# A hybrid pooling and retention block on one core: order of the wide and narrow products in the up projection, and place of the gating multiplies

## The chip, the cores and the metric

One Trainium2 chip, one of its cores. The metric is the device time of one execution, in microseconds (us). Engines: PE is TensorE's matmuls, PEld its weight loads, DVE VectorE, ACT ScalarE, SP the engine that issues the transfers.

## What is computed

One layer of a streaming encoder on 256 tokens of width 2048, float32 throughout:

```
u = RMSNorm(h)
z = u @ W_in   -> pool | q | k | v | ret_gate | gate_pool | gate_ret
yA = PoolBranch(pool) @ P_pool
yB = (swish(ret_gate) * GroupNorm(Retention(q, k, v))) @ P_ret
h = h + (sigmoid(gate_pool) * yA + sigmoid(gate_ret) * yB) @ W_out
h = h + ConvGLU(RMSNorm(h))     up: 2048 -> 2 x 5632, causal conv of 3 and SiLU on
                                the gate half, times the other half, down: 5632 -> 2048
out = RMSNorm_final(h)
```

The change touches two places: the line of `h` that gates and adds `yA` and `yB`, and the up projection in ConvGLU.

## The kernel before, in words

Every float32 operand of a large product is split in two: `hi`, rounded to the matmul's format, and `lo`, the rest. ScalarE writes `hi` (line 82), VectorE subtracts to get `lo` (line 83). A product is then three matmuls: hi·hi, hi·lo, lo·hi.

Weights come in transfers of 1 MB (`load_split`, line 94: a raw tile of 128 x 2048, buffers: 3) and are split in two halves of 128 x 1024 each (`hi` and `lo`, 3 buffers each). `product` (line 213) makes a 256 x 512 block of a result: for each group of four 128-row steps it loads one raw tile, and per step and token block `tb` (two of 128 tokens) does the three matmuls of 512 columns (lines 90 to 92) into `ps[tb]`. The two `ps` are halves of one tile of the pool `acc`, which has two buffers.

The code is written in program order; a scheduling layer then sets the order of each engine's instructions and the semaphores, and every engine runs its own list in order. Work that TensorE should meet in between (transposes, score products) stands in the queue `side`, from which `tick()` takes one piece at set places.

*Gating (lines 459 to 486).* For each of four column blocks `nb`: the pool projection's product into `psp` (48 matmuls), then the retention projection's into `psr` (96 matmuls), then per token block three operations on VectorE: `psp` times gate (line 471), `psr` times gate (472), their sum (473). The sum is transposed later, on a tick of the next product. `psp` and `psr` take the two buffers of `acc` in turns, so the next block's `psp` needs the buffer of this block's `psp`.

*Up projection (lines 544 to 580).* 44 blocks `j`, each with two halves (gate and up, 128 columns of the result each). The weights are the stationary operand here, and the normed hidden state moves: `hview(kt)` holds 256 columns of its hi part and, beside them, 256 of its lo part. So one wide matmul of 512 columns (weight hi against both parts) and one narrow one of 256 (weight lo against the hi part) make up a step:

```python
pe.matmul(o[half], wh[:, s], both, start=kt == 0, stop=False)
pe.matmul(o[half][:, :T], wl[:, s], both[:, :T], start=False, stop=False)
```

A half-block is 16 such steps into one bank `o[half]`: 16 wide (line 556, the last one line 560) and 16 narrow (557, 559). The loop runs over halves, and in each over the two weight tiles `hf` (8 steps each); in block 0 it runs over `hf` first. After the products the epilogue adds the two parts (ScalarE line 565, VectorE 568), scales (570), does the convolution (574 to 576), SiLU (577) and the product of the halves (578), and splits the result (lines 82, 83). The residual adds of the last output column block (line 520), their transposes (511) and the second norm (lines 526 to 536) still run during block 0; line 534 makes a scaled identity that a small matmul (535) spreads over partitions.

Of the kernel before, what the change touches and what calls it, by code (L numbers as in the profile page):

```python
# [13 lines left out]
ALU = mybir.AluOpType  # L14
PSUM = bass.MemoryType.PSUM

P = 128
D = 2048
T = 256
TB = 2  # L20
KT = D // P
NB = 512
# [21 lines left out]
def tile_block(ctx: ExitStack, tc: tile.TileContext, ins, out):  # L44
    nc = tc.nc
    pe, act, dve, sp = nc.tensor, nc.scalar, nc.vector, nc.sync
# [12 lines left out]
    def nm(base):  # L59
        counter[0] += 1  # L60
        return f"{base}_{counter[0]}"

    def unit(dt=F32):
        return units.tile([P, UNIT], dt, tag="u", name=nm("u"))

    def t2k(n=512, dt=F32):
        return tmp.tile([P, n], dt, tag="t2k", name=nm("t"), padded_shape=[P, 512])

    def acc_pair():

        a = acc.tile([P, 2 * NB], F32, tag="acc", name=nm("acc"))
        return [a[:, i * NB : (i + 1) * NB] for i in range(2)]

    def aux_tile():
        return aux.tile([P, NB], F32, tag="aux", name=nm("aux"))
# [5 lines left out]
    def split(hi, lo, src):  # L81
        act.activation(hi, src, AF.Copy)  # L82
        dve.tensor_tensor(lo, src, plain(hi), ALU.subtract)  # L83
# [5 lines left out]
    def mm3(o, ah, al, bh, bl, start, stop):  # L89
        pe.matmul(o, ah, bh, start=start, stop=False)  # L90
        pe.matmul(o, ah, bl, start=False, stop=False)  # L91
        pe.matmul(o, al, bh, start=False, stop=stop)  # L92

    def load_split(src):

        raw = wraw.tile([P, 2048], F32, tag="raw", name=nm("raw"))
        sp.dma_start(raw, src)
        got = []
        for h in range(2):
            r = raw[:, h * 1024 : (h + 1) * 1024]  # L100
            hi = wsplit.tile([P, 1024], F32R, tag="hi", name=nm("hi"))
            lo = wsplit.tile([P, 1024], F32R, tag="lo", name=nm("lo"))
            split(hi, lo, r)
            got.append((hi, lo))
        return got
# [18 lines left out]
    def tick():  # L124
        if side:
            side.popleft()()
# [20 lines left out]
    def kview(pair, kt):  # L147
        return pair[kt // 8][:, (kt % 8) * T : (kt % 8 + 1) * T]
# [6 lines left out]
    for n in (1, 1) + (2,) * 7:  # L155
# [5 lines left out]
        w2 = raws[g][:, at * NB : (at + n) * NB]  # L161
# [8 lines left out]
        for j in range(n):  # L170
            o = slice((at + j) % 2 * NB, ((at + j) % 2 + 1) * NB)
# [11 lines left out]
    def vec(c):  # L183
        return vecs[:, c : c + 1]
# [28 lines left out]
    def product(src, start, nk, lhs_h, lhs_l, ready=None, bank=None):  # L213

        ps = [bank() for _ in range(TB)] if bank else acc_pair()
        for g in range(nk // 4):
            halves = [ready[g, 0], ready[g, 1]] if ready else load_split(src[start + g])
            for hf, (wh, wl) in enumerate(halves):
                for j in range(2):
                    kt = g * 4 + hf * 2 + j  # L220
                    s = slice(j * NB, (j + 1) * NB)
                    for tb in range(TB):
                        ah = lhs_h(kt)[:, tb * P : (tb + 1) * P]
                        al = lhs_l(kt)[:, tb * P : (tb + 1) * P]
                        mm3(ps[tb], ah, al, wh[:, s], wl[:, s], kt == 0, kt == nk - 1)
            tick()
        return ps
# [220 lines left out]
    sgp = [unit(), unit()]  # L448
    sgr = [unit(), unit()]
# [9 lines left out]
    for nb in range(4):  # L459
        psp = product(  # L460
            ins["w_pool_proj"],
            nb * 2,
            8,
            lambda k: mix_h[:, k * T : (k + 1) * T],
            lambda k: mix_l[:, k * T : (k + 1) * T],
        )
        psr = product(ins["w_ret_proj"], nb * 4, KT, lambda k: kview(ret_h, k), lambda k: kview(ret_l, k))
        for tb in range(TB):
            a, b = t2k(), t2k()
            s = slice(tb * 1024 + (nb % 2) * NB, tb * 1024 + (nb % 2 + 1) * NB)  # L470
            dve.tensor_tensor(a, psp[tb], sgp[nb // 2][:, s], ALU.mult)  # L471
            dve.tensor_tensor(b, psr[tb], sgr[nb // 2][:, s], ALU.mult)  # L472
            dve.tensor_tensor(a, a, b, ALU.add)

            def turn(a=a, nb=nb, tb=tb):
                pt = aux_tile()
                for c in range(4):
                    pe.transpose(pt[:, c * P : (c + 1) * P], a[:, c * P : (c + 1) * P], ident)  # L478
                n0 = (nb % 2) * 4
                dst = [  # L480
                    x[nb // 2].rearrange("p (k t) -> p k t", t=T)[:, n0 : n0 + 4, tb * P : (tb + 1) * P]
                    for x in (mg_h, mg_l)
                ]
                split(dst[0], dst[1], pt.rearrange("p (c t) -> p c t", t=P))

            side.append(turn)
# [5 lines left out]
    def hview(kt):  # L492
        return ht[kt // 4][:, (kt % 4) * 2 * T : (kt % 4 + 1) * 2 * T]
# [22 lines left out]
    for nb in range(4):  # L516
        ps = product(ins["w_out"], nb * 4, KT, lambda k: kview(mg_h, k), lambda k: kview(mg_l, k))
        s = slice(nb * NB, (nb + 1) * NB)
# [25 lines left out]
    for j in range(NFF):  # L544

        o = acc_pair()
        w2 = [load_split(ins["w_up"][2 * j + half]) for half in range(2)]
        order = [(half, hf) for half in range(2) for hf in range(2)]
        for half, hf in sorted(order, key=lambda x: x[1]) if j == 0 else order:
            wh, wl = w2[half][hf]  # L550
            for i in range(8):
                kt = hf * 8 + i
                s = slice(i * P, (i + 1) * P)
                both = hview(kt)
                if kt < KT - 1:
                    pe.matmul(o[half], wh[:, s], both, start=kt == 0, stop=False)  # L556
                    pe.matmul(o[half][:, :T], wl[:, s], both[:, :T], start=False, stop=False)  # L557
                else:
                    pe.matmul(o[half][:, :T], wl[:, s], both[:, :T], start=False, stop=False)  # L559
                    pe.matmul(o[half], wh[:, s], both, start=False, stop=True)  # L560
                if i % 4 == 3:
                    tick()
        small_part, gu = t2k(), t2k()
        for half in range(2):
            act.activation(small_part[:, half * T : (half + 1) * T], o[half][:, T:], AF.Copy)  # L565
        for half in range(2):
            h2 = slice(half * T, (half + 1) * T)
            dve.tensor_tensor(gu[:, h2], o[half][:, :T], small_part[:, h2], ALU.add)  # L568
        gv = gu.rearrange("p (s t) -> p s t", s=2)
        dve.tensor_tensor(gv, gv, rb.unsqueeze(1).broadcast_to([P, 2, T]), ALU.mult)  # L570
        g, u = gu[:, :T], gu[:, T:]
        c = t2k(T)
        w = [vec(C_CONVW + i * NFF + j) for i in range(3)]
        dve.tensor_scalar(c, g, w[2], None, ALU.mult)
        dve.scalar_tensor_tensor(c[:, 1:], g[:, : T - 1], w[1], c[:, 1:], ALU.mult, ALU.add)
        dve.scalar_tensor_tensor(c[:, 2:], g[:, : T - 2], w[0], c[:, 2:], ALU.mult, ALU.add)
        act.activation(c, c, AF.Silu, bias=vec(C_CONVB + j))
        dve.tensor_tensor(c, c, u, ALU.mult)  # L578
        s = slice((j % 8) * T, (j % 8 + 1) * T)
        split(ah[j // 8][:, s], al[j // 8][:, s], c)  # L580
# [5 lines left out]
    part = small.tile([P, TB], F32, tag="part", name="part", bufs=1)  # L586
# [51 lines left out]
    for g in range(NFF // 4):  # L638
        if g * 4 >= NFF - LAST and g == NFF // 4 - 1:
# [4 lines left out]
            for h2 in range(2):  # L644
                s = slice(h2 * 1024, (h2 + 1) * 1024)
# [4 lines left out]
        for hf, (wh, wl) in enumerate(halves):  # L650
            for j in range(2):
                kt = g * 4 + hf * 2 + j
                s = slice(j * NB, (j + 1) * NB)
# [97 lines left out]
```

## Time and profile before

| | |
|---|---|
| time, median of 3 runs | 1500.37 us (1499.43 to 1500.54) |
| profiled execution | 1500.19 us, span 1498.4 us |
| TensorE busy | 1480.2 us (99%), 7286 matmuls |
| VectorE busy | 911.1 us (61%) |
| ScalarE busy | 698.2 us (47%) |
| transfers | 287.01 MB, mean 192 GB/s |

The span is the profiler's from the first to the last instruction; the time has some 2 us around it. Matmuls are pipelined, so the duration in a row is longer than the distance from one start to the next, and the ends overlap; what TensorE's stream takes is read from the starts. A row of the timeline gives start and duration in us, engine, line, operation, result <- operands, and in brackets the idle time before it and what ended it.

### The profile page before, as it was taken

How to read it: one execution, taken by the hardware profiler on the slowest of the kernel's cores; microseconds unless marked ns; L12 is line 12 of the kernel's file. 1: busy time of each engine (PE TensorE's matmuls, PEld its weight loads, DVE VectorE, ACT ScalarE, POOL GpSimd, SP SyncE). 2: the span in 40 equal slices, each digit the busy share in tenths (PEclk: the TensorE clock that was granted, in tenths of full speed). 3: DMA queues.
4: the chain of work that ended last, by engine and by line, in shares of the span. 5: the costliest groups of instructions: out<-in, count | busy, mean ns of one | idle time of the engine just before them, and what ended most of it. 6: DMA issues, size and time to landing. Idle time of an engine off the chain costs nothing.

```text
span 1498.4 us, 18277 instructions
## 1 busy us (share of the span) xinstructions
PE 1480.2 (99%) x7286; PEld 1243.5 (83%) x7286; DVE 911.1 (61%) x1229; ACT 698.2 (47%) x899; POOL 0.2 (0%) x4
## 2 busy tenths in 40 slices
PE   9999999999999999999999999999999999999997
PEld 6888888888888877778888888888888888888886
DVE  5765865675444455555577777777766766445454
ACT  6545444455444433334455444444454444344343
POOL 0000000000000000000000000000000000000000
PEclk9999999999999999999999999999999999999999
DMA  9654555464555555565545555555555555555553
GB/s 336 208 204 161 189 192 195 165 212 178 171 194 197 197 180 185 197 211 182 191 174 193 176 194 185 182 196 178 187 194 176 193 187 211 195 194 196 197 196 113
DMA packets 42710, 287.01 MB, mean 192 GB/s; under 512 B 4993, under 2 KB 5633, under 8 KB 9089
## 3 DMA queue, kind: packets, MB, share of 16 engines
q1 hardware_dynamic: 42624, 285.84, 54.9%
q8 instruction: 57, 0.93, 0.2%
q14 instruction: 29, 0.23, 0.0%
HBM read 283.73 MB, written 2.10 MB: 191 GB/s over the span
## 4 chain that ended last, share of the span: by engine, by line
PE 98%; DVE 1%; DMA 1%; SPq 0%; issue 0%; ACT 0%; ACTq 0%
PE acc L90 21%; PE acc L92 20%; PE acc L91 20%; PE acc L556 20%; PE acc L557 10%; PE acc L560 1%; PE aux L91 1%; PE aux L92 1%; PE aux L90 1%; PE acc L559 1%; DMA raw<-in_w_in 1%; PE aux L248 0%; PE aux L478 0%; PE aux L341 0%; DVE lo L83 0%; DVE t L472 0%
## 5 line engine op out<-in xcount | busy, mean ns | idle before, releaser
L83 DVE TENSOR_TENSOR lo<-raw,hi 128x1024 fp32r<-128x1024 f32 (+1 forms) x526 | 634.6, 1208 | 460.3 <-ACT hi L82 460.2
L82 ACT ACTIVATE hi<-raw 128x1024 fp32r<-128x1024 f32 (+1 forms) x526 | 549.3, 1046 | 588.6 <-PE acc L92 438.8
L90 PE MATMUL acc<-hi,u 128*128 128x512 f32 x1336 | 524.1, 392 | 5.9 <-DVE t L471 5.9
L92 PE MATMUL acc<-hi,u 128*128 128x512 f32 x1336 | 520.6, 390 | 0.0
L91 PE MATMUL acc<-lo,u 128*128 128x512 f32 x1336 | 520.0, 389 | 0.0
L556 PE MATMUL acc<-u,hi 128*128 128x512 f32 x1320 | 470.2, 399 | 0.0
L557 PE MATMUL acc<-u,lo 128*128 128x256 f32 x1320 | 370.8, 281 | 0.0
L90 PEld LDWEIGHTS acc<-hi,u 128*128 128x128 f32 x1336 | 250.9, 188 | 57.8 <-ACT hi L82 7.5
L556 PEld LDWEIGHTS acc<-u,hi 128*128 128x128 f32 x1320 | 248.0, 188 | 56.9
L92 PEld LDWEIGHTS acc<-hi,u 128*128 128x128 f32 x1336 | 250.7, 188 | 53.3
L91 PEld LDWEIGHTS acc<-lo,u 128*128 128x128 f32 x1336 | 251.1, 188 | 50.3
L557 PEld LDWEIGHTS acc<-u,lo 128*128 128x128 f32 x1320 | 249.3, 189 | 4.2
L565 ACT ACTIVATE t<-acc 128x256 f32<-128x256 f32 x88 | 29.1, 382 | 70.5 <-PE acc L560 70.5
L568 DVE TENSOR_TENSOR t<-acc,t 128x256 f32<-128x256 f32 x88 | 33.3, 420 | 45.5 <-ACT t L565 45.5
L82 ACT ACTIVATE u<-t 128x256 fp32r<-128x256 f32 x44 | 18.3, 417 | 51.6 <-DVE t L578 51.6
L560 PE MATMUL acc<-u,hi 128*128 128x512 f32 x88 | 35.2, 400 | 0.0
L570 DVE TENSOR_TENSOR t<-t,rb 128x512 f32<-128x512 f32 x44 | 30.5, 693 | 1.5
L83 DVE TENSOR_TENSOR u<-t,u 128x256 fp32r<-128x256 f32 x44 | 18.6, 424 | 19.3 <-ACT u L82 19.3
L86 ACT ACTIVATE u<-aux,vecs 128x256 fp32r<-128x256 f32 x40 | 18.7, 469 | 23.6 <-DVE u L87 22.7
L559 PE MATMUL acc<-u,lo 128*128 128x256 f32 x88 | 24.9, 283 | 0.0
L87 DVE SCALAR_TENSOR_TENSOR u<-aux,vecs,u 128x256 fp32r<-128x256 f32 x40 | 19.1, 481 | 8.7 <-ACT u L86 8.7
L271 ACT ACTIVATE u<-acc,y 128x512 f32<-128x512 f32 x24 | 15.2, 686 | 17.0 <-PE acc L92 17.0
(132 smaller groups left out, 538.9 us busy)
## 6 DMA issues: line engine op xcount, KB each, us to landing
raw<-in_w_up SPq DMA_DIRECT2D x88, 1024.0 KB, 4.9
raw<-in_w_in SPq DMA_DIRECT2D x84, 1024.0 KB, 4.9
raw<-in_w_down SPq DMA_DIRECT2D x44, 1024.0 KB, 4.9
raw<-in_w_ret_proj SPq DMA_DIRECT2D x16, 1024.0 KB, 4.9
raw<-in_w_out SPq DMA_DIRECT2D x16, 1024.0 KB, 4.9
raw<-in_w_pool_proj SPq DMA_DIRECT2D x8, 1024.0 KB, 5.0
u<-in_x SPq DMA_DIRECT2D x4, 1024.0 KB, 7.7
raw<-in_w_in SPq DMA_DIRECT2D x7, 512.0 KB, 8.5
```

Of the source, the lines that this page charges most:

```text
L82: act.activation(hi, src, AF.Copy)
L83: dve.tensor_tensor(lo, src, plain(hi), ALU.subtract)
L90: pe.matmul(o, ah, bh, start=start, stop=False)
L91: pe.matmul(o, ah, bl, start=False, stop=False)
L92: pe.matmul(o, al, bh, start=False, stop=stop)
L556: pe.matmul(o[half], wh[:, s], both, start=kt == 0, stop=False)
L557: pe.matmul(o[half][:, :T], wl[:, s], both[:, :T], start=False, stop=False)
L559: pe.matmul(o[half][:, :T], wl[:, s], both[:, :T], start=False, stop=False)
L560: pe.matmul(o[half], wh[:, s], both, start=False, stop=True)
L565: act.activation(small_part[:, half * T : (half + 1) * T], o[half][:, T:], AF.Copy)
L568: dve.tensor_tensor(gu[:, h2], o[half][:, :T], small_part[:, h2], ALU.add)
L570: dve.tensor_tensor(gv, gv, rb.unsqueeze(1).broadcast_to([P, 2, T]), ALU.mult)
```

## The change

In the gating, the two multiplies of `psp` are written ahead of the retention projection, into tiles of their own (`gated`). In the up projection, `wide` and `narrow` become functions of a half and a weight tile. In blocks 1 to 43 each half does its 16 wide products and then its 16 narrow ones; in block 0 the wide ones of both halves, then the narrow ones of both, for the first weight tile and then for the second. The last matmul of a half is now a narrow one. `tick()` is called in the wide products only, after every fourth.

```diff
@@ gating
+        cols = [slice(tb * 1024 + (nb % 2) * NB, tb * 1024 + (nb % 2 + 1) * NB) for tb in range(TB)]
+        gated = [t2k() for _ in range(TB)]
+        for tb in range(TB):
+            dve.tensor_tensor(gated[tb], psp[tb], sgp[nb // 2][:, cols[tb]], ALU.mult)
         psr = product(ins["w_ret_proj"], nb * 4, KT, lambda k: kview(ret_h, k), lambda k: kview(ret_l, k))
         for tb in range(TB):
-            a, b = t2k(), t2k()
-            s = slice(tb * 1024 + (nb % 2) * NB, tb * 1024 + (nb % 2 + 1) * NB)
-            dve.tensor_tensor(a, psp[tb], sgp[nb // 2][:, s], ALU.mult)
-            dve.tensor_tensor(b, psr[tb], sgr[nb // 2][:, s], ALU.mult)
+            a, b = gated[tb], t2k()
+            dve.tensor_tensor(b, psr[tb], sgr[nb // 2][:, cols[tb]], ALU.mult)
             dve.tensor_tensor(a, a, b, ALU.add)
@@ up projection
-        order = [(half, hf) for half in range(2) for hf in range(2)]
-        for half, hf in sorted(order, key=lambda x: x[1]) if j == 0 else order:
-            wh, wl = w2[half][hf]
+        def wide(half, hf):
             for i in range(8):
                 kt = hf * 8 + i
-                s = slice(i * P, (i + 1) * P)
-                both = hview(kt)
-                if kt < KT - 1:
-                    pe.matmul(o[half], wh[:, s], both, start=kt == 0, stop=False)
-                    pe.matmul(o[half][:, :T], wl[:, s], both[:, :T], start=False, stop=False)
-                else:
-                    pe.matmul(o[half][:, :T], wl[:, s], both[:, :T], start=False, stop=False)
-                    pe.matmul(o[half], wh[:, s], both, start=False, stop=True)
+                pe.matmul(o[half], w2[half][hf][0][:, i * P : (i + 1) * P], hview(kt), start=kt == 0, stop=False)
                 if i % 4 == 3:
                     tick()
+
+        def narrow(half, hf):
+            for i in range(8):
+                kt = hf * 8 + i
+                wl = w2[half][hf][1][:, i * P : (i + 1) * P]
+                pe.matmul(o[half][:, :T], wl, hview(kt)[:, :T], start=False, stop=kt == KT - 1)
+
+        if j == 0:
+            for hf in range(2):
+                for part in (wide, narrow):
+                    for half in range(2):
+                        part(half, hf)
+        else:
+            for half in range(2):
+                for part in (wide, narrow):
+                    for hf in range(2):
+                        part(half, hf)
```

How it moves instructions is seen in the order of the built program; a number behind a name is that of the tile. First VectorE at the end of the first column block's pool projection (`acc_3949` is `psp`; the `lo` tiles on both sides belong to the retention projection's weights):

```order
-L83 TENSOR_TENSOR lo_4026<-raw_4019,hi_4025 128x1024 [waits Activation_49]
-L471 TENSOR_TENSOR t_4155<-acc_3949,u_2697 128x512 [waits PE_49]
-L83 TENSOR_TENSOR lo_4056<-raw_4053,hi_4055 128x1024 [waits DMAHW4_49,Activation_49]
...
+L83 TENSOR_TENSOR lo_4030<-raw_4023,hi_4029 128x1024 [waits Activation_49]
+L470 TENSOR_TENSOR t_4018<-acc_3949,u_2697 128x512 [waits PE_49]
+L470 TENSOR_TENSOR t_4019<-acc_3949,u_2697 128x512
+L83 TENSOR_TENSOR lo_4060<-raw_4057,hi_4059 128x1024 [waits DMAHW4_49,Activation_49]
```

Both multiplies now stand there, where before only the first token block's did. Some ten splits later, at the end of the retention projection (`acc_4018` before, `acc_4022` after, is `psr`):

```order
-L472 TENSOR_TENSOR t_4156<-acc_4018,u_2699 128x512 [waits PE_49]
-L471 TENSOR_TENSOR t_4160<-acc_3949,u_2697 128x512
-L473 TENSOR_TENSOR t_4155<-t_4155,t_4156 128x512 [waits DVE_49]
-L472 TENSOR_TENSOR t_4161<-acc_4018,u_2699 128x512
+L474 TENSOR_TENSOR t_4159<-acc_4022,u_2699 128x512 [waits PE_49]
+L474 TENSOR_TENSOR t_4162<-acc_4022,u_2699 128x512
+L475 TENSOR_TENSOR t_4018<-t_4018,t_4159 128x512 [waits DVE_49]
+L475 TENSOR_TENSOR t_4019<-t_4019,t_4162 128x512 [waits DVE_49]
```

The second multiply of `psp` (line 471 on `acc_3949`), which stood behind line 472 here, is gone from this place. Last, TensorE in one half-block of the up projection, before:

```order
L556 MATMUL acc_6463<-u_4855,hi_6466 128x512
L557 MATMUL acc_6463<-u_4855,lo_6467 128x256
L556 MATMUL acc_6463<-u_4855,hi_6466 128x512
L557 MATMUL acc_6463<-u_4855,lo_6467 128x256
...
L559 MATMUL acc_6463<-u_4858,lo_6471 128x256
L560 MATMUL acc_6463<-u_4858,hi_6470 128x512
```

and the whole of it after:

```order
L555 MATMUL acc_6463<-u_4855,hi_6466 128x512 x4
L555 MATMUL acc_6463<-u_4856,hi_6466 128x512 x4
L555 MATMUL acc_6463<-u_4857,hi_6470 128x512 x4
L555 MATMUL acc_6463<-u_4858,hi_6470 128x512 x4
L563 MATMUL acc_6463<-u_4855,lo_6467 128x256 x4
L563 MATMUL acc_6463<-u_4856,lo_6467 128x256 x4
L563 MATMUL acc_6463<-u_4857,lo_6471 128x256 x4
L563 MATMUL acc_6463<-u_4858,lo_6471 128x256 x4
```

Sixteen of a kind stand in a row; the two `lo` tiles of the half are read only after both of its `hi` tiles.

## Rows read from the trace of the kernel before

**Rows 1.** The page: TensorE's line of part 1, and part 4's shares by engine.
```profile
PE 1480.2 (99%) x7286; PEld 1243.5 (83%) x7286; DVE 911.1 (61%) x1229; ACT 698.2 (47%) x899; POOL 0.2 (0%) x4
...
PE 98%; DVE 1%; DMA 1%; SPq 0%; issue 0%; ACT 0%; ACTq 0%
```
**Rows 2.** Busy us by stretch (PE, PEld, DVE, ACT, POOL), clock, DMA share, GB/s.
```profile
900.00:1000.00 100.00, 100.00 (x568) 86.73 (x567) 71.48 (x108) 49.21 (x72) 0.00 (x0) 1.00 0.55 190
```
**Rows 3.** Waits of TensorE: total us, times, longest.
```profile
PE acc L90 <- DVE t L471: 5.9, 4, 1.5
```
**Rows 4.** Timeline of TensorE, from a retention projection to the next pool projection.
```profile
552.03 0.39 PE L92 MATMUL acc<-hi,u 128*128 128x512 f32 x1
553.89 0.47 PE L90 MATMUL acc<-hi,u 128*128 128x512 f32 x1 [1.47 <-DVE t L471]
...
555.36 0.39 PE L90 MATMUL acc<-hi,u 128*128 128x512 f32 x1
```
**Rows 5.** Timeline of VectorE at the same place.
```profile
552.45 0.69 DVE L472 TENSOR_TENSOR t<-acc,u 128x512 f32<-128x512 f32 x1 [0.40 <-PE acc L92]
553.06 0.68 DVE L471 TENSOR_TENSOR t<-acc,u 128x512 f32<-128x512 f32 x1
```
**Rows 6.** Timeline of TensorE, a half-block of the up projection: first pair, next half-block.
```profile
905.23 0.40 PE L556 MATMUL acc<-u,hi 128*128 128x512 f32 x1
905.46 0.28 PE L557 MATMUL acc<-u,lo 128*128 128x256 f32 x1
...
910.88 0.40 PE L556 MATMUL acc<-u,hi 128*128 128x512 f32 x1
```
**Rows 7.** Timeline of TensorE: starts of block 1, its second half, block 2, down projection.
```profile
764.00 0.40 PE L556 MATMUL acc<-u,hi 128*128 128x512 f32 x1
...
769.64 0.40 PE L556 MATMUL acc<-u,hi 128*128 128x512 f32 x1
...
775.20 0.39 PE L556 MATMUL acc<-u,hi 128*128 128x512 f32 x1
...
1250.08 0.40 PE L90 MATMUL acc<-hi,u 128*128 128x512 f32 x1
```
**Rows 8.** Timeline of TensorE: pool mixing's 12 narrow products, then wide ones.
```profile
367.41 0.28 PE L90 MATMUL aux<-t,u 128*128 128x256 f32 x1
...
368.84 0.40 PE L90 MATMUL acc<-hi,u 128*128 128x512 f32 x1
...
370.00 0.39 PE L92 MATMUL acc<-hi,u 128*128 128x512 f32 x1
...
372.49 0.39 PE L91 MATMUL acc<-lo,u 128*128 128x512 f32 x1
```
**Rows 9.** Timeline of TensorE in block 0: first transpose, second norm's small matmuls.
```profile
752.45 0.27 PE L511 MATMUL aux<-ident,u 128*128 128x128 f32 x1
...
759.59 0.46 PE L535 MATMUL aux<-dg,ones 128*128 128x128 f32 x2 [0.18 <-DVE dg L534]
```
**Rows 10.** Timeline of VectorE in block 0: the two residual adds.
```profile
751.24 1.29 DVE L520 TENSOR_TENSOR u<-acc,u 128x512 f32<-128x512 f32 x2 [0.34 <-PE acc L92]
```
**Rows 11.** Timeline of VectorE in the up projection: from the epilogue's start to line 576.
```profile
900.47 0.76 DVE L568 TENSOR_TENSOR t<-acc,t 128x256 f32<-128x256 f32 x2 [1.03 <-ACT t L565]
...
901.87 1.22 DVE L83 TENSOR_TENSOR lo<-raw,hi 128x1024 fp32r<-128x1024 f32 x1
...
904.92 0.48 DVE L576 SCALAR_TENSOR_TENSOR t<-t,vecs,t 128x254 f32<-128x254 f32 x1
```
**Rows 12.** Timeline of TensorE's weight loads in the pool mixing.
```profile
367.41 0.19 PEld L91 LDWEIGHTS aux<-t,u 128*128 128x128 f32 x1
367.53 0.19 PEld L92 LDWEIGHTS aux<-t,u 128*128 128x128 f32 x1
```
**Rows 13.** Timeline of TensorE: the pool branch's window products (256 and 128 columns).
```profile
374.31 0.40 PE L406 MATMUL aux<-u,u 128*128 128x256 f32 x2
...
375.18 0.45 PE L90 MATMUL acc<-hi,u 128*128 128x512 f32 x1
```

## The prediction

> **What bounds the kernel now.** I read the page's first part and its chain before anything else. TensorE is busy for 1480.2 us of a 1498.4 us span, and 98% of the chain that ended last is TensorE [rows 1]. So nothing counts here but the time that TensorE's own stream takes: where it stands still, and how far apart its matmuls start. The granted clock is no question: in a stretch of the up projection it is 1.00, the 2.4 GHz level, with TensorE busy all the time [rows 2], so nothing can come back from there.
>
> The list of waits says where TensorE stands still after its start: 4 times, 5.9 us in all, for the gating multiply of line 471 [rows 3]. One of these places in order of time: the last matmul of a retention projection starts at 552.03, the first of the next pool projection not before 553.89 [rows 4]. In between VectorE does line 472 and then line 471 for the second token block [rows 5]. The pool projection's accumulator is one buffer for both token blocks, and acc has two buffers, so the next product but one needs it back; its last reader, line 471, stands on VectorE behind line 472, which needs the retention projection's end.
>
> The other place is the distance of matmuls in the up projection. There a wide product (512 columns) and a narrow one (256) alternate; a half-block of 16 pairs goes from 905.23 to 910.88, 5.65 us or 353 ns a pair [rows 6]. The same 16 pairs take 5.56 us in one single half-block, the second of block 1, from 769.64 to 775.20; from there to the first product after the up projection at 1250.08 lie 84 half-blocks, 474.88 / 84 = 5.653 us each [rows 7]. So the same instructions in the same order run at two rhythms, and all but one of the last 85 half-blocks run at the slower.
>
> What do wide and narrow products take among their own kind? In the pool branch's mixing 12 narrow products stand in a row, each with new weights, and then wide ones follow: 12 narrow from 367.41 to 368.84, 1.43 us, and the next 16 wide from 368.84 to 372.49, 3.65 us, the turn from one kind to the other included [rows 8]. That is nearly the pattern that the change makes.
>
> **The change part by part.** *Up projection.* No instruction is added or removed: 1408 wide and 1408 narrow products, the same loads, splits and copies; only TensorE's order changes. A half-block becomes 16 wide, then 16 narrow. From rows 8: wide 3.65 us; narrow 1.43 us for 12 and 4 more at the burst's mean of 0.12, together 1.91; sum 5.56 us. That is the quick rhythm's 5.56 too. Against 5.653: 0.093 us less in each of 84 half-blocks, 7.8 us; with block 1's first half (764.00 to 769.64, 5.64) 7.9 us. The best bound: wide products that begin at once at their settled distance. From 370.00 to 372.49 lie 11 starts, 0.2264 us each, so 16 would take 3.62; 0.03 us less in some 85 half-blocks is 2.5 us more gained. The worst: a wide product in a long chain keeps the up projection's rhythm, and nothing is gained.
>
> *Block 0* has its own order (wide of both halves, narrow of both, twice), among which the last transposes and the second norm's small matmuls stand. Now TensorE waits 0.18 us there for the scaled identity of line 534 [rows 9], and the transposes need the two residual adds, which take VectorE from 751.24 to 752.5 [rows 10]. TensorE reaches the first transpose 0.5 us earlier than now, at about 751.95, since 4 wide products stand ahead of it in place of 4 pairs; the first add ends at about 751.9, and the second token block's transposes are now placed three wide products after the first one, so a wait of up to 0.2 us can come at either place. Against it, some pairs of this block get shorter too. I take 0, bounds -0.3 and +0.4.
>
> *Where the weights come from.* The three hi and three lo buffers are held differently: hi buffers come free earlier, the lo buffers of a half only as its narrow products run. The tightest is the second half's first lo tile: its buffer is free only when the last narrow product of the block before ends. On VectorE it stands ahead of that block's epilogue. From 900.47 to 905.40 VectorE did two splits and the epilogue up to line 576, 4.9 us; a split is 1.2 [rows 11], so the epilogue is 2.5. After the change: split 1.2, epilogue 2.5, then the last lo tile when its buffer is free, at 3.65 + 0.96 = 4.6 us into the block, done at about 5.9. The narrow products that need it start 1 us ahead of the block's end, 10.1 us into it. That leaves 4 us; VectorE is busy for 71% in that stretch now [rows 2], and its work is the same. If the cover went, each us of lateness would cost 44 us. Weight transfers keep their order on SP's queue.
>
> *Gating.* The two multiplies of the pool half go ahead of the retention projection on VectorE and run in its first us; at the end line 474 and 475 remain (4 operations as before, now 2 + 2). The wait of TensorE at the next product goes. Its price is more than the 1.47 us that the wait list counts: from 552.03 to 555.36 there are 7 starts, 3.33 us; 7 at the settled 0.226 us would be 1.59, so 1.74 us, since the first products after a stop come slower as well. 4 x 1.74 = 7.0 us (by the wait list alone 5.9, my other bound). What is late next? VectorE's splits: behind the two early multiplies (0.69 us each) waits the second group of retention weights. Its buffer frees at that same moment, so it ends 1.4 + 1.2 us after the pool projection, and is needed 24 x 0.226 = 5.4 us after it. At the product's end four operations of 0.69 stand before the next split, done after 4.2 us, needed again after 5.4. Little spare, but enough; I put 0.1 us on it.
>
> *Sum.* 7.9 + 7.0 + 0 - 0.1 = 14.8 us. The profiled execution took 1500.19 us (span 1498.4), 0.2 under the median of 1500.37; 1500.37 - 14.8 = **1485.6 us**. Its own bounds: 2.5 us less by the settled distance and 0.3 by block 0, and rounded, 1483; 1.1 us more with 5.9 for the gating and 0.4 for block 0, 1487.
>
> A rule of the Trainium skill speaks against half of this. "TensorE: Matmul & The Clock Gate", section "Back-to-back issue gap", gives the gap of a warm matmul as its columns at 2.4 GHz and 2.5 ns more, with no term for what stands beside it: some 325 ns for a pair in any order, and nothing to gain by grouping. The trace differs, with 353 and 347 ns for the same pairs [rows 6, 7].
>
> **The rivals.** *Order is neutral (chance 0.10).* A product's start distance belongs to its own size and its accumulator, and the single quick half-block is a stray. Then the up projection stays at 5.65 us a half and the gating alone counts: 1500.4 - 7.0 + 0.1 = 1493.5. For it: the products of rows 8 write other accumulators, with other operands. Against it: rows 7, where the same products take 5.56. This is the case that the rule just named would make.
>
> *The stall moves (0.04).* VectorE's splits come late behind the early multiplies and TensorE waits as long in the retention projection: 1500.4 - 7.9 = 1492.5. For it: spare time of 1.2 us at one place; against it: the sum above.
>
> *Slower: loads bound the narrow chain (0.03).* A weight load takes 0.19 us, more than a narrow product's 0.12 [rows 12]. Among wide products a load has time. If in a chain of 16 the loads could not overlap one another, narrow products would start 0.19 us apart: 1408 x 0.07 = 99 us more, so 1500.4 - 7.0 + 99 = 1592. It decides from the point where loads come less often than every 0.12 us; at 0.13 the grouping is already a loss of 14 - 7.9 = 6 us. Against it: loads start 0.12 us apart in rows 12, and 12 products stand so in rows 8, and 8 products with new weights, half of them of 128 columns, start within 374.31 to 375.18, 0.11 us each [rows 13].
>
> That the change doesn't do what it says is excluded by the order of the built program, shown above.
>
> **How the numbers follow.** The forecast has 0.83. With its own bounds it lies between 1483 and 1487. To leave out no more than 2 in 10 the range must reach over the two weaker gains, to 1493.8. A measurement of this kernel tells about 0.2%, 3 us, from no change. All cases but the slow one gain over 6 us: faster 0.95; the slow one 0.03; 0.02 for a gain that is eaten up by waits I have not seen.
>
> **What would show it.** In the profile of the changed kernel: no wait of TensorE for the gating; the two early multiplies right behind the pool projection's end. Half-blocks at 5.56 us, narrow products 0.12 apart and wide ones 0.227 after the first few. No wait of the narrow products for a lo tile. A half-block at 5.65 would show the order neutral; narrow starts over 0.125 us apart, or waits for line 83, would make the forecast wrong.

## The result and the profile after

The changed kernel takes 1486.05 us, median of 4 runs (1485.32 to 1486.44); the kernel before took 1500.07 beside it (1499.43 to 1500.54). The ratio is 0.9906, 95% interval 0.9889 to 0.9923: 14.0 us faster. Forecast were 1485.6 us.

Nothing else became the bound. TensorE's line of the page's first part and the chain of the changed kernel, to be set against [rows 1]:

```profile
PE 1472.3 (99%) x7286; PEld 1244.8 (84%) x7286; DVE 911.1 (61%) x1229; ACT 707.7 (48%) x899; POOL 0.2 (0%) x4
...
PE 98%; DMA 1%; SPq 0%; DVE 0%; ACT 0%; issue 0%; ACTq 0%
```

The same 7286 matmuls, TensorE still 98% of the chain, in a span of 1484.3 us. The list of its waits (total us, times, longest) no longer has the gating of [rows 3]; what is left belongs to the first products of the kernel:

```profile
PE aux L90 <- ACT hi L82: 1.7, 3, 0.9
PE aux L139 <- DVE warm L134: 1.2, 1, 1.2
PE aux L91 <- DVE lo L83: 0.2, 1, 0.2
```

The place of [rows 4] in the changed kernel's timeline of TensorE, the end of a retention projection (line 92) and the start of the next pool projection (line 90):

```profile
552.08 0.39 PE L92 MATMUL acc<-hi,u 128*128 128x512 f32 x1
552.30 0.39 PE L90 MATMUL acc<-hi,u 128*128 128x512 f32 x1
```

0.22 us apart where there were 1.86. VectorE around it, from the end of the pool projection on (line 470 the early multiplies, 474 and 475 what remains at the end, line 83 the next split):

```profile
530.75 1.29 DVE L470 TENSOR_TENSOR t<-acc,u 128x512 f32<-128x512 f32 x2 [0.40 <-PE acc L92]
...
552.50 1.29 DVE L474 TENSOR_TENSOR t<-acc,u 128x512 f32<-128x512 f32 x2 [0.40 <-PE acc L92]
553.71 1.28 DVE L475 TENSOR_TENSOR t<-t,t 128x512 f32<-128x512 f32 x2
554.91 1.22 DVE L83 TENSOR_TENSOR lo<-raw,hi 128x1024 fp32r<-128x1024 f32 x1
```

The multiplies run as soon as the pool projection is done. The split behind the four last operations ends at 554.91 + 1.22 = 556.13, and its first user comes after 24 products of 0.227 us, at about 557.7. The spare time is some 1.6 us, more than the 1.2 us of the prediction, and it was enough.

Now the stream itself. Two rows of TensorE's timeline in the kernel before: a product just ahead of the first pool projection, and the start of the up projection:

```profile
517.80 0.39 PE L91 MATMUL acc<-lo,u 128*128 128x512 f32 x1
...
751.04 0.39 PE L556 MATMUL acc<-u,hi 128*128 128x512 f32 x1
```

and in the changed kernel the same two, then the starts of block 1, of one half-block (wide, narrow, next wide) and of the down projection:

```profile
517.85 0.39 PE L91 MATMUL acc<-lo,u 128*128 128x512 f32 x1
...
744.08 1.07 PE L555 MATMUL acc<-u,hi 128*128 128x512 f32 x4
...
757.18 3.82 PE L555 MATMUL acc<-u,hi 128*128 128x512 f32 x16
...
901.92 3.82 PE L555 MATMUL acc<-u,hi 128*128 128x512 f32 x16
905.57 2.08 PE L563 MATMUL acc<-u,lo 128*128 128x256 f32 x16
907.48 3.82 PE L555 MATMUL acc<-u,hi 128*128 128x512 f32 x16
...
1235.92 0.40 PE L90 MATMUL acc<-hi,u 128*128 128x512 f32 x1
```

| stretch of TensorE's stream | before, us | after, us | difference |
|---|---|---|---|
| gating and output projection | 751.04 - 517.80 = 233.24 | 744.08 - 517.85 = 226.23 | -7.01 |
| block 0 of the up projection | 764.00 - 751.04 = 12.96 | 757.18 - 744.08 = 13.10 | +0.14 |
| blocks 1 to 43 | 1250.08 - 764.00 = 486.08 | 1235.92 - 757.18 = 478.74 | -7.34 |

(764.00 and 1250.08 are in [rows 7].) A half-block goes from 5.65 to 478.74 / 86 = 5.567 us: 16 wide products in 3.65 us and 16 narrow ones in 1.91. The three differences sum to -14.21 us; the spans differ by 14.1.

### The profile page after: what moved, and what is told of

It reads as the page before. It is cut to its first block, busy times and chain, and to the rows that moved or that the text cites. A ratio compares the mean times of both kernels' runs of the same rounds, so it can differ in the third digit from the quotient of the medians.

```text
span 1484.3 us, 18232 instructions
## 1 busy us (share of the span) xinstructions
PE 1472.3 (99%) x7286; PEld 1244.8 (84%) x7286; DVE 911.1 (61%) x1229; ACT 707.7 (48%) x899; POOL 0.2 (0%) x4
## 4 chain that ended last, share of the span: by engine, by line
PE 98%; DMA 1%; SPq 0%; DVE 0%; ACT 0%; issue 0%; ACTq 0%
PE acc L555 22%; PE acc L90 21%; PE acc L92 21%; PE acc L91 21%; PE acc L563 11%; PE aux L91 1%; PE aux L92 1%; PE aux L90 1%; DMA raw<-in_w_in 1%; PE aux L513 0%; PE aux L248 0%; PE aux L480 0%; PE aux L341 0%; PE aux L406 0%; SPq L160 0%; PE aux L410 0%
## 5 line engine op out<-in xcount | busy, mean ns | idle before, releaser
L555 PE MATMUL acc<-u,hi 128*128 128x512 f32 x1408 | 337.1, 391 | 0.0
L555 PEld LDWEIGHTS acc<-u,hi 128*128 128x128 f32 x1408 | 258.6, 188 | 49.8
L563 PEld LDWEIGHTS acc<-u,lo 128*128 128x128 f32 x1408 | 180.5, 191 | 6.9
L563 PE MATMUL acc<-u,lo 128*128 128x256 f32 x1408 | 182.6, 283 | 0.0
L587 DVE SCALAR_TENSOR_TENSOR t<-t,vecs,t 128x255 f32<-128x255 f32 x44 | 21.3, 484 | 1.6
L588 DVE SCALAR_TENSOR_TENSOR t<-t,vecs,t 128x254 f32<-128x254 f32 x44 | 21.3, 483 | 1.5
L589 ACT ACTIVATE t<-t,vecs 128x256 f32<-128x256 f32 x44 | 21.6, 491 | 0.0
```

The source lines that it names most:

```text
L555: pe.matmul(o[half], w2[half][hf][0][:, i * P : (i + 1) * P], hview(kt), start=kt == 0, stop=False)
L563: pe.matmul(o[half][:, :T], wl, hview(kt)[:, :T], start=False, stop=kt == KT - 1)
```

## The experiments

**Each part alone.** `up_only` has the old gating and the new up projection, `gate_only` the new gating and the old up projection.

> The kernel before with the up projection's new order alone. Theory (two separate gains): the up projection takes 491.8 us as in the changed kernel, against 499.0 before, and the 4 stops of TensorE at the gating stay with 5.9 us in the list of waits: 1500.1 - 7.2 = 1492.9 us. Rival (the parts hang together, the faster up projection comes from what the gating leaves behind, such as an earlier start of the weight transfers): more than 1494, or the half-blocks not at 5.57 us.

> The kernel before with the early multiplies alone. Theory: the 4 stops go, half-blocks of the up projection stay at 5.65 us, 1500.1 - 7.0 = 1493.1 us. Rival (only the 5.9 us of the list of waits come back, the slow first products after a stop do not): 1494.2. Rival (the stop comes back later as a wait for weights): 1500, with waits for line 83 in the retention projection.

Measured: `up_only` 1492.75 us, ratio 0.9951 (0.9936 to 0.9966); `gate_only` 1493.35 us, ratio 0.9955 (0.9940 to 0.9970), with 1500.14 for the kernel before. TensorE's waits for VectorE in `up_only`:

```profile
PE acc L90 <- DVE t L471: 5.9, 4, 1.5
```

This row is not in `gate_only`. The starts of its timeline at the places of the table (the product ahead of the first pool projection, up projection, down projection), and between them the first two half-blocks of block 1:

```profile
518.08 0.39 PE L91 MATMUL acc<-lo,u 128*128 128x512 f32 x1
...
744.30 0.39 PE L559 MATMUL acc<-u,hi 128*128 128x512 f32 x1
...
757.25 0.40 PE L559 MATMUL acc<-u,hi 128*128 128x512 f32 x1
...
762.81 0.39 PE L559 MATMUL acc<-u,hi 128*128 128x512 f32 x1
...
1243.34 0.40 PE L90 MATMUL acc<-hi,u 128*128 128x512 f32 x1
```

The stretch with the gating takes 226.22 us, as in the changed kernel, the up projection 499.04, as in the kernel before. `up_only`'s rows at the same places:

```profile
517.49 0.39 PE L91 MATMUL acc<-lo,u 128*128 128x512 f32 x1
...
750.72 0.62 PE L553 MATMUL acc<-u,hi 128*128 128x512 f32 x2
...
1242.56 0.40 PE L90 MATMUL acc<-hi,u 128*128 128x512 f32 x1
```

Here it is the other way: 233.23 and 491.84. So the two gains are separate and add, 7.0 and 7.2 us, and the rivals to both fall: the stops bring back more than the listed 5.9 us, and they do not return as a wait for weights.

**Is it the grouping, or the swapped pair?** The old order alternates, but swaps the last pair of each half, so that two narrow and then two wide products meet there. And one of its half-blocks was quick without any grouping. `strict` alternates without the swap:

```diff
+            for half in range(2):
+                for kt in range(KT):
+                    one(half, kt, True, kt == 0, False)
+                    one(half, kt, False, False, kt == KT - 1)
```

> The changed kernel, but blocks 1 to 43 of the up projection alternate wide and narrow strictly, 16 pairs a half, without the swap of the last pair that the kernel before had. Theory A (each turn from a kind to the other costs time): half-blocks at 5.65 us as before, 86 x 0.086 = 7.4 us over the changed kernel, 1493.5 us. Theory B (alternation as such runs at the quick rhythm of 347 ns a pair; the swap at a half's end throws it into the slow one): half-blocks at 5.55 to 5.57 us, 1486 us.

Measured: 1493.52 us, ratio 0.9957 (0.9940 to 0.9973). TensorE's timeline of `strict`: start of block 1, five pairs later on, start of the down projection:

```profile
757.25 0.40 PE L569 MATMUL acc<-u,hi 128*128 128x512 f32 x1
...
902.82 0.40 PE L569 MATMUL acc<-u,hi 128*128 128x512 f32 x1
903.06 0.28 PE L571 MATMUL acc<-u,lo 128*128 128x256 f32 x1
903.18 0.40 PE L569 MATMUL acc<-u,hi 128*128 128x512 f32 x1
...
904.59 0.40 PE L569 MATMUL acc<-u,hi 128*128 128x512 f32 x1
...
1243.44 0.40 PE L90 MATMUL acc<-hi,u 128*128 128x512 f32 x1
```

(1243.44 - 757.25) / 86 = 5.653 us a half, the old 5.653 to the last digit; five pairs take 1.77 us, 354 ns each. Theory A holds for every half-block of `strict`, and the swap is innocent. But the quick half-block is no stray of one execution: `gate_only`, with the old order, has one too, the first of block 1, 762.81 - 757.25 = 5.56 us. So alternation can keep the quick pace for 16 pairs; what ends it, no run shows.

**How large must the groups be?** `twos` and `fours` have runs of 2 and 4 of a kind, `both` the 32 wide products of both halves and then the 32 narrow ones.

> The changed kernel with two wide and two narrow products in turns in blocks 1 to 43, 8 runs of each kind in a half in place of 1 (the kernel before has 16). Theory A, with a cost in proportion to the turns: 5.567 + 7/15 x 0.086 = 5.607 us a half, 1486.05 + 3.4 = 1489.5 us. Theory B: a rhythm is either there or not, half-blocks at 5.55 to 5.57 or at 5.65.

> The changed kernel with runs of 4 wide and 4 narrow products in blocks 1 to 43. Since pairs of two took 5.573 us a half and sixteens 5.567: rhythm theory, 5.55 to 5.60 us a half and 1485 to 1489 us. Rival (a turn costs the 20 ns of slow wide products seen after each narrow run of 16): 4 turns, 5.547 + 0.080 = 5.627 us a half, 1491 us.

> The changed kernel with the wide products of both halves of a block in a row, 32 of them, and then the 32 narrow ones, in blocks 1 to 43: half as many turns. Theory: each turn less saves the 20 ns that the products after it lose, 43 x 0.020 = 0.9 us, 1485.2 us, and no wait for the lo tiles, whose buffers are held longer. Rival: the fourth lo tile of a block, whose buffer frees only with the block's first 8 narrow products, is late: a wait for line 83 in each block, each us of it 43 us.

Measured: `twos` 1485.52 us (one run), `fours` 1490.09 us (one run), `both` 1484.49 us (1484.39 to 1485.10), ratio 0.9894 (0.9878 to 0.9911). Block 1 and the down projection start in `twos` at

```profile
756.06 0.63 PE L569 MATMUL acc<-u,hi 128*128 128x512 f32 x2
...
1235.37 0.40 PE L90 MATMUL acc<-hi,u 128*128 128x512 f32 x1
```

and in `fours` at

```profile
757.20 0.40 PE L569 MATMUL acc<-u,hi 128*128 128x512 f32 x1
...
1239.94 0.40 PE L90 MATMUL acc<-hi,u 128*128 128x512 f32 x1
```

The start of block 1 in `both`, and its down projection:

```profile
756.38 7.44 PE L555 MATMUL acc<-u,hi 128*128 128x512 f32 x32
763.66 4.00 PE L563 MATMUL acc<-u,lo 128*128 128x256 f32 x32
...
1234.26 0.40 PE L90 MATMUL acc<-hi,u 128*128 128x512 f32 x1
```

The last two columns of the table are the mean distances from the start of a wide and of a narrow product to the next start, over blocks 1 to 43 of each trace; 16 times their sum is the half-block.

| runs of a kind | a half-block, us | wide, ns | narrow, ns |
|---|---|---|---|
| 1 (`strict`) | 5.653 | 236.4 | 116.9 |
| 2 (`twos`) | (1235.37 - 756.06) / 86 = 5.573 | 233.1 | 115.2 |
| 4 (`fours`) | (1239.94 - 757.20) / 86 = 5.613 | 232.3 | 118.5 |
| 16 (the change) | 5.567 | 228.4 | 119.5 |
| 32 (`both`) | (1234.26 - 756.38) / 86 = 5.557 | 227.5 | 119.8 |

The cost does not go with the number of turns: `twos` turns eight times as often as the changed kernel and is nearly as quick (its single time is the lower one because its block 1 began 1.1 us earlier, at 756.06 against 757.18), `fours` lies in the middle, outside of what the rhythm theory allowed it (5.55 to 5.60) and below the rival's 5.627. Both expectations for `fours` missed. From 16 to 32 the saving is what was expected, and no wait for a lo tile came.

The distances show what the odd order of the table is made of: a turn has two sides. In the changed kernel the first five wide products behind a turn take 233, 236, 228, 233 and 231 ns to the next start, and all further ones 227; the first narrow products take 113 and 119 ns, and the further ones 120. So wide products lose some 5 ns each until they settle, and the first narrow ones gain. In strict alternation no wide product settles. In runs of two the wide ones still lose 6 ns each, but every narrow one gains some 5, which nearly makes up for it; in runs of four the wide ones lose as much and most of that gain is gone. The same slow start stands behind a stop: behind the one at 552.03 in the kernel before, the products from 553.89 on take 307, 233, 236, 224, 231, 236, 228, 232 and 231 ns, and then 227.

**How near was the slow rival?** Narrow products of 192 and 128 columns:

```diff
+                m = T if j == 0 else 192
+                pe.matmul(o[half][:, :m], wl, hview(kt)[:, :m], start=False, stop=kt == KT - 1)
```

> The changed kernel, whose narrow products in blocks 1 to 43 have 192 columns in place of 256; the part of the lo weights for the other 64 tokens is left out there. Theory C (a narrow product in a chain takes its columns at 2.4 GHz and the 13 ns that wide and narrow ones show beside theirs: 226.7 - 213.3, 120 - 106.7): 93 ns apart, a half-block 5.567 - 16 x 0.027 = 5.14 us, 1486.05 - 86 x 0.427 = 1449 us. Rival D (a chain of narrow products is bound by something that each product needs once, its weight load or its issue, at 0.11 to 0.12 us): 110 to 120 ns apart, 5.41 to 5.57 us a half, 1472 to 1486 us.

> The same with 128 columns, the lo weights' part for 128 tokens left out in blocks 1 to 43. Theory C: 67 ns apart, a half-block 5.567 - 16 x 0.053 = 4.71 us, 1412 us. Rival D: 110 to 120 ns apart, 1472 to 1486 us. A floor between would stand at the same distance in both kernels, or show from 128 columns on alone.

Measured: `narrow192` 1474.73 us, `narrow128` 1478.81 us, one run each. TensorE's timeline of `narrow192`:

```profile
903.87 3.82 PE L555 MATMUL acc<-u,hi 128*128 128x512 f32 x16
907.53 1.93 PE L564 MATMUL acc<-u,lo 128*128 128x192 f32 x16
909.30 3.83 PE L555 MATMUL acc<-u,hi 128*128 128x512 f32 x16
```

and of `narrow128`:

```profile
905.04 3.90 PE L555 MATMUL acc<-u,hi 128*128 128x512 f32 x16
908.78 1.90 PE L564 MATMUL acc<-u,lo 128*128 128x128 f32 x16
910.52 3.90 PE L555 MATMUL acc<-u,hi 128*128 128x512 f32 x16
```

16 narrow products take 1.77 and 1.74 us, 0.11 us each, with 192 as with 128 columns; theory C wanted 1.49 and 1.07. So here a chain of products with new weights settles at about 0.11 us each with 192 as with 128 columns, and with 128 columns the wide ones behind them even lose 0.08 us (3.74 for 16 in place of 3.66). Only the first distance of a chain is shorter, 0.086 and 0.057 us. The 256 columns of this kernel, 0.120 us, lie just above that floor.

The weight loads of `narrow128` point to what sets it:

```profile
909.12 0.19 PEld L564 LDWEIGHTS acc<-u,lo 128*128 128x128 f32 x1
909.23 0.19 PEld L564 LDWEIGHTS acc<-u,lo 128*128 128x128 f32 x1
```

From the fourth load of a chain on they start every 112 ns to within 1 ns, in both runs, while the products beside them start 109 to 117 ns apart, and no two of these loads start less than 108 ns apart where the first two products of a chain start 57 ns apart. This points to the loads as what keeps the pace, with the products following them; whether a load itself or its issue takes the 112 ns, these runs don't tell. The Trainium skill, "TensorE: Matmul & The Clock Gate", section "LDWEIGHTS (loading the stationary operand)", gives a load's time as its columns / 1.2, for 128 columns an estimate of 107 ns. The 112 ns here lie close to it. The rows of single loads show 0.19 us [rows 12], but as they start 0.11 us apart they overlap.

**Why does alternation cost?** The floor suggested a theory: a narrow product of 120 ns leaves the next load hardly any room, so a wide one behind it starts late. With 384 columns there is room. `group384` groups, `strict384` alternates.

> The changed kernel with narrow products of 384 columns in blocks 1 to 43: the lo weights also meet 128 columns of the hidden state's lo part, which no other kernel here computes. A control for the next one. Columns and 13 ns: 173 ns apart, 16 x (226.7 + 173.3) = 6.40 us a half-block, 1486.05 + 86 x 0.833 = 1557.7 us.

> The same 384 columns, wide and narrow in strict alternation as in the run strict. Theory (alternation costs because a narrow product of 120 ns leaves the next weight load hardly more than the 112 ns that the runs narrow192 and narrow128 showed; with 173 ns there is room): half-blocks within 0.02 us of group384's. Rival (each turn between two sizes costs, whatever the sizes): 16 x 6.6 ns = 0.1 us more a half, 9 us more in all, as strict stood to the changed kernel.

Measured: 1563.33 and 1575.63 us, one run each. TensorE's timeline of `group384`:

```profile
902.96 2.96 PE L564 MATMUL acc<-u,lo 128*128 128x384 f32 x16
905.76 3.83 PE L555 MATMUL acc<-u,hi 128*128 128x512 f32 x16
909.43 2.96 PE L564 MATMUL acc<-u,lo 128*128 128x384 f32 x16
```

and of `strict384`:

```profile
902.62 0.40 PE L569 MATMUL acc<-u,hi 128*128 128x512 f32 x1
902.86 0.34 PE L571 MATMUL acc<-u,lo 128*128 128x384 f32 x1
...
904.28 0.40 PE L569 MATMUL acc<-u,hi 128*128 128x512 f32 x1
```

Grouped, 16 pairs take 2.80 + 3.67 = 6.47 us, 0.07 more than the columns and 13 ns had given. Alternating, 4 pairs take 1.66 us, some 0.415 each where the grouped ones take 6.47 / 16 = 0.404 (by the times, 12.3 / 86 = 0.143 us a half over the grouped kernel). The theory falls: with 0.175 us per narrow product, well over the 0.112 of a load, alternation costs not less than with 256 columns (0.086 us a half) but more. The starts of `strict` already spoke against it. There the wide product starts 0.12 us behind its narrow one (903.06, 903.18), no later than in a chain; the one that comes late is the narrow product behind the wide one, 0.24 us after it (902.82, 903.06). In `strict384` too nearly all of the cost stands behind the wide products: 237.5 ns to the next start in place of 229.2, and 175.8 in place of 175.0 behind the narrow ones. The rival, that alternating two sizes costs whatever the sizes, is nearer, though its 0.1 was too low. That it is the size that matters, and not the change of weights, is argued and not tested: in lines 90 to 92 each product loads weights of its own too, and the wide ones settle at 0.2264 us [rows 8].

**The two best side by side.**

> The changed kernel once more, on the same chip as the next run, to set the two side by side: 1485 to 1486.5 us, up projection 491.84 us long, as in its profile.

> The version with 32 wide and 32 narrow products in a row once more. Theory (43 turns fewer at 20 ns, which its first profile shows as 490.99 us for the up projection against 491.84): 0.85 us under after_again. The first products of a run start up to 1 us earlier or later from one execution to the next, so by times alone the order of the two may not be told.

Measured, with 1500.25 for the kernel before: 1485.39 us (1484.89 to 1486.43), ratio 0.9903 (0.9889 to 0.9918), and 1485.46 us (1484.70 to 1486.94), ratio 0.9901 (0.9885 to 0.9918). Starts of the up and down projection in `after_again`:

```profile
744.41 1.07 PE L555 MATMUL acc<-u,hi 128*128 128x512 f32 x4
...
1236.26 0.40 PE L90 MATMUL acc<-hi,u 128*128 128x512 f32 x1
```

and in `both_again`:

```profile
745.79 0.39 PE L555 MATMUL acc<-u,hi 128*128 128x512 f32 x1
...
1236.78 0.40 PE L90 MATMUL acc<-hi,u 128*128 128x512 f32 x1
```

The up projection takes 491.85 and 490.99 us, so the 0.86 us are there; but this execution of `both` reached the up projection, which comes after the same code, 1.38 us later, which more than takes them back. By times the two can't be told apart; `both` is better by its stream alone.

## Why the prediction was right

*What bounds the kernel* held: TensorE's stream before and after, 98% of the chain, and what its starts say of the stretches is what the time did, 14.2 us against 14.0. That the forecast time is only 0.5 us off has some luck in it: the forecast gain of 14.8 us was 0.8 too large, and the kernel before, run beside the changed one, took 0.3 us less than the 1500.37 that the forecast started from.

*Gating*: forecast 7.0 us, measured 7.01. Taking the price from the starts rather than from the list of waits made the difference between 5.9 and 7.0, and `gate_only` shows it alone. The reason that the prediction gave for the difference, slower first products after a stop, is less than half of it. A stop cost 7.01 / 4 = 1.75 us, 0.28 more than the 1.47 in the list. The list counts from the end of the row before, which is 0.39 us long, while unhindered the next product starts 0.227 us after that row's start: 0.16 of the 0.28 us. Only the other 0.12 are the slower products. The 0.1 us put on late splits was not needed: no wait for line 83 stands there.

*Up projection*: forecast 7.9 us, measured 7.34 in blocks 1 to 43. The mechanism was right, the term a little too large: a half-block takes 5.567 us where the rows of the pool branch, read to hundredths, gave 3.65 + 1.91 = 5.56. 0.007 us in 86 half-blocks are the missing 0.6 us. The rows themselves were right: unrounded, their starts give 3.654 + 1.912 = 5.566. *Block 0*: forecast 0, measured +0.14, within its bounds; what makes it, no row here shows.

*Weights*: 4 us of spare time were worked out for the tightest lo tile, and no wait for one appeared, not even in `both`, which holds the lo buffers longer.

*Rivals*: order neutral fell (5.567 us a half, and `up_only`'s 7.2 us); the stall moved nowhere; loads did not bound the narrow chain, since 0.120 us is above the floor of about 0.11. That rival was nearer than its chance of 0.03 suggests: [rows 13] had already shown products at 0.11 us in the mean with 128 and 256 columns mixed, which is about the floor, and the prediction read it only as proof that loads can follow so closely. It is a mean alone: the single starts there lie 0.06 to 0.17 us apart. The 325 ns a pair that the prediction worked out from the Trainium skill came in no order: wide and narrow products settle at 226.7 and 120 ns, 13 ns over their columns at 2.4 GHz. In "TensorE: Matmul & The Clock Gate", section "Back-to-back issue gap", the Trainium skill gives that gap for an isolated matmul, and says that in a stream the loads share in the spacing, so it spoke less firmly against the change than the prediction took it to.

What stays open is why alternation costs. The prediction did not explain the two rhythms, it only used them; the load theory that followed fell in `strict384`. That grouping removes the cost is shown, and so is where the cost stands: in the wide products that follow a turn or a stop, up to about the fifth or the ninth. Why those start late is not.

## What to carry to other kernels

Where TensorE is the whole chain, read its starts, not its durations or its list of waits: a stop costs more than its listed idle time (here 1.75 us for 1.47), and alternating two sizes of product can cost 1.5% of a stretch that looks fully busy (5.653 us a half-block in place of 5.567). Give an accumulator back by moving its last reader ahead of the product that doesn't need it. When small products with new weights each are put in a row, measure their floor first, here about 0.11 us a product: 192 columns already stood on it, and cutting them to 128 gained nothing more.

## What the runs showed that was not expected

- Wide and narrow float32 products in strict alternation settle at 353 to 354 ns a pair, in runs of two at 5.573 / 16 = 348 ns, in runs of four at 351 ns, in runs of 16 at 348 ns. Behind a turn or a stop, wide products take 224 to 236 ns to the next start before they settle at 227.
- 16 products of 192 and of 128 columns with new weights take 1.77 and 1.74 us: they no longer follow the columns, and the loads start every 112 ns. With 128 columns the kernel as a whole is slower than with 192, 1478.81 to 1474.73 us, as the wide products behind the chain lose more.
- The stretches of TensorE's stream repeat to 0.01 us from one execution to the next (226.22 and 226.23, 499.04 twice, 491.84, 491.84 and 491.85); what differs between executions of a kernel lies ahead of them, up to 2.5 us (`both` reaches the up projection at 743.27 in one profile and at 745.79 in the other).
